# Down-weight sums in two places, and hand-overs written out by operation, in a two-layer encoder

## The chip, the core and the metric

One Trainium2 chip, of which the kernel uses one core. The metric is the device time of one launch in microseconds: 2563.12 as the median of three runs (2561.14 to 2563.65). One further execution was taken by the profiler; every duration and window below comes from that one.

## The reference

Two layers over 512 tokens of width 1024, all in float32. Each layer: a half-step FFN, a mixer, a second half-step FFN, each between two RMS norms.

```python
y = swiglu(rmsnorm(h, ffn1_pre_g[l]), ffn1_w_gu[l], ffn1_w_down[l])
h = h + 0.5 * rmsnorm(y, ffn1_post_g[l])
u = rmsnorm(h, mix_pre_g[l])
qa, ka, va, qb, kb, vb, qc, kc, vc, gl = jnp.split(u @ w_in[l], split_at, axis=-1)
...
yb = jnp.einsum('bsnc,ncd->bsnd', branches, w_branch[l])
merged = jnp.sum(sigmoid(gl + b_gate[l]) * yb, axis=2)
h = h + rmsnorm(merged @ w_out[l], mix_post_g[l])
y = swiglu(rmsnorm(h, ffn2_pre_g[l]), ffn2_w_gu[l], ffn2_w_down[l])
h = h + 0.5 * rmsnorm(y, ffn2_post_g[l])
```

`swiglu` is silu(gate) times up, times the down weights; the inner width is 2816. The three branches are a neighbourhood attention (a), a sliding-window attention with rotary (b) and a differential attention with rotary (c).

## The kernel before, in words

**Products in three.** Every float32 operand is split into a high part (a rounding copy by ScalarE) and a low part (the remainder, by VectorE), and a product is three matmuls: high by high, high by low, low by high (`mm3`, L298 to L300, and `unit` in the down part, L1014). Weights stream from DRAM in tiles of 512 KB through three raw buffers (`wr`, L186), are split by L199 and L200, and are used in the order of the list `order`.

**An FFN** has a gate and up part and a down part. Both use a scheme of seven products in place of eight on 2x2 blocks. In the gate and up part the first columns (`plain`: six in the first FFN, four in the others) go by ordinary products; then 16 or 18 groups of seven products each follow (L796, 84 matmuls of 256 columns per group), with `p1, p7, p6, p4, p2, p5, p3` in a written order. The sums of weight blocks that the seven products need are made by VectorE in each group (`sum13` L649, `sum2` L668, `sum4` L678).

**The down part** (from L868) works through units: `seq` lists kinds 1, 7, n2, 6, 4, n1, 2, 5, 3 with four units each (three in n1 and n2, which are ordinary products of the remaining rows). A unit of the seven takes one 512 KB tile of weights, split by `prep` (L892 and L893) some units ahead (`preps(s + 5)`), loaded by SP (`load`, L882) into three raw buffers and a ring of four. Kinds 7, 6, 5, 3 need sums of weight blocks: s3 = 21 + 11, s2 = s3 + 22, s1 = 21 + 22, s4 = s2 + 12. Before, all four are made in DRAM by transfers: a copy, and a second transfer that adds in flight (`sum_up`, L246 to L261; 32 transfers of 512 KB per FFN). They are issued on POOL, in small lots, each behind a one-column copy (`paced`, the mark of L265) that waits for a tile of the current work: for the first FFN of layer 0 two at a time within its own gate and up part (`beside`), for the second FFN of a layer and the first of the next layer spread over the mixer that lies ahead. Layer 0's mixer carries 64 such transfers, layer 1's 32.

The products land in PSUM banks for token blocks of 128: `a` and `c` in four banks, `b` in the seeds of the gate and up part, `d` and `e` in two more. Their sums are four quarters of y (two token blocks by 512 columns each): v11 (from b), v21, v22 and v12, kept in SBUF. `jobs` says at which unit such a step is issued.

**The hand-over** (`Handover`, L409) turns y into the next stage's operand, token block by token block: `take` squares and sums (ScalarE) and multiplies by the gain (VectorE, L436); `merge` makes the reciprocal root (L440 to L442), adds to the residual h (L450), squares h (L453), writes h to DRAM (`kept`, L468), and scales (L473); `turn` transposes on TensorE (L483) and splits the result (L487, L488; L492 keeps a plain copy). After the last FFN it transposes h instead (L458) and writes the output. `begin` starts the next stage with its first three column blocks, first for token blocks 0 and 1, then for 2 and 3, with hooks between its steps. The last mixer product (`w_out`) has a hand-over of the same class.

**What sets the order.** Outside `ordered()` a planner orders the instructions of each engine by its own costs. Inside (from the end of the gate and up part to the end of `begin`, and from `w_out` to the end of its `begin`) TensorE, ScalarE and VectorE keep the written order. Every engine takes its instructions in order, and so do the queues of SP and POOL. In the mixer POOL also does the rotary's multiplication (L1267), on a copy whose 32-row pieces SP has moved (`sh`, L1264), and adds the branches.

Of the kernel before, what the change touches and what calls it, by code (L numbers as in the profile page):

```python
# [16 lines left out]
P = 128  # L17
L = 2
# [91 lines left out]
def encoder_kernel(ctx: ExitStack, tc: tile.TileContext, order, xT, wts, cols, rows, rpb, consts, tables, out):  # L110
# [135 lines left out]
    def sum_up(l, which):  # L246

        steps = []

        def begin_sum(key, old, u):  # L250
            t = dr.tile([P, 2, T], F32, tag="sum", name=nm("sum"), bufs=L * 2 * 4 * (KS // 2))
            G.dma_start(t, down[l, which, (old, u)] if old == "21" else sums[l, which, (old, u)])
            sums[l, which, (key, u)] = t

        def add_to(key, more, u):
            G.dma_start(sums[l, which, (key, u)], down[l, which, (more, u)], accum_op=ALU.add, max_dma_last_dim=4096)

        for key, old, more in (("s3", "21", "11"), ("s2", "s3", "22"), ("s1", "21", "22"), ("s4", "s2", "12")):
            steps.extend((lambda key=key, old=old, u=u: begin_sum(key, old, u)) for u in range(KS // 2))
            steps.extend((lambda key=key, more=more, u=u: add_to(key, more, u)) for u in range(KS // 2))  # L260
        return steps  # L261
# [107 lines left out]
    def begin(X, first, spare, tags, hooks=(), between=None):  # L369
# [6 lines left out]
        assert len(held) <= len(spare)  # L376
        accs, ws = dense(first, X, tags, 0, hooks=dict(hooks))
        if between:
            between()
        dense(first, X, (), 1, accs, ws)  # L380
        return accs
# [27 lines left out]
    class Handover:  # L409


        def __init__(self, l, post, factors, following, gains, hold, value, raw, tags):
            self.tags = tags
# [8 lines left out]
            self.ss = [small("sh", 2, 8) for _ in range(NT)]  # L422
# [10 lines left out]
        def take(self, tb, n, src):  # L433
            junk = big("t", name="junk")
            A.activation(junk, src, AF.Square, accum_out=self.ss[tb][:, n : n + 1])
            V.tensor_tensor(out=self.value(tb, n), in0=src, in1=self.g1[n], op=ALU.mult)  # L436

        def rms(self, ss):
            r = small("rh", 1, 8)
            V.tensor_tensor(out=r, in0=ss[:, 0:1], in1=ss[:, 1:2], op=ALU.add)  # L440
            A.activation(r, r, AF.Sqrt, scale=1.0 / D, bias=epst)
            V.reciprocal(out=r, in_=r)  # L442
            return r

        def merge(self, tb):
            r = self.rms(self.ss[tb])
            s2 = small("sh", 2, 8)
            for n in range(2):
                y, h = self.value(tb, n), self.hold(tb, n)
                V.scalar_tensor_tensor(out=h, in0=y, scalar=r, in1=h, op0=ALU.mult, op1=ALU.add)  # L450
                if self.following:
                    junk = big("t", name="junk")
                    A.activation(junk, h, AF.Square, accum_out=s2[:, n : n + 1])  # L453
            if not self.following:
                for n in range(2):
                    tp = bank(self.tags[n])
                    for k in range(HB):
                        PE.transpose(tp[:, k * P : (k + 1) * P], self.hold(tb, n)[:, k * P : (k + 1) * P], ident)  # L458
                    o = self.value(tb, n)
                    (A.activation(o, tp, AF.Copy) if n else V.tensor_copy(o, tp))  # L460
                    nc.sync.dma_start(
                        out[n * T : (n + 1) * T, tb * P : (tb + 1) * P].rearrange("(k p) t -> p k t", p=P),
                        o.rearrange("p (k t) -> p k t", k=HB),
                    )
                return
            d = dr.tile([P, D], F32, tag="kept", name=nm("kept"), bufs=2 * NT)
            for n in range(2):
                nc.sync.dma_start(d[:, n * T : (n + 1) * T], self.hold(tb, n))  # L468
            kept[tb] = d
            r = self.rms(s2)  # L470
            for n in range(2):
                x = self.value(tb, n)
                V.scalar_tensor_tensor(out=x, in0=self.hold(tb, n), scalar=r, in1=self.g2[n], op0=ALU.mult, op1=ALU.mult)  # L473

        def turn(self, tb):
            if self.X is None:
                self.X = Operand(self.raw)
            raws = []
            for n in range(2):
                x = self.value(tb, n)  # L480
                tp = bank(self.tags[n])
                for k in range(HB):
                    PE.transpose(tp[:, k * P : (k + 1) * P], x[:, k * P : (k + 1) * P], ident)  # L483
                src = tp.rearrange("p (k t) -> p k t", k=HB)
# [4 lines left out]
                if self.raw:  # L489
                    raws.append((self.X.raw[n][:, tb // 2, :, ts], src))  # L490
            for o, src in raws:
                A.activation(o, src, AF.Copy)  # L492
# [22 lines left out]
    def ffn(l, which, X, accs):  # L515
# [37 lines left out]
        if first:  # L553
            stream["stop"] = len(order) // HB + 4 * plain
            accs = begin(X.blocks, firsts_of(l, 0), [spare("ht1"), spare("lt1")], ("mm", "at"), (), between)
            stream["beside"] = sum_up(l, which)
# [315 lines left out]
        done = {"load": 0, "prep": 0}  # L872
        place_of = {"1": "11", "2": "12", "4": "22", "7": "s3", "6": "s2", "5": "s1", "3": "s4", "n1": "n1", "n2": "n2"}

        def load(s):
            kind, u = seq[s]
            if s < UNITS:
                wraw[s] = sb.tile([P, 2, T], F32, tag="wr", name=nm("wr"), bufs=BUFS["wr"])
            else:
                wraw[s] = z(("ht3", "lt3", "ht2", "lt2")[s % 4], F32)  # L880
            key = place_of[kind], u
            nc.sync.dma_start(wraw[s], (sums if key[0][0] == "s" else down)[l, which, key])  # L882

        def prep(s):
            kind, u = seq[s]
            src = wraw.pop(s)
# [4 lines left out]
            else:  # L891
                A.activation(h, src, AF.Copy)  # L892
                V.tensor_tensor(out=q, in0=src, in1=f(h), op=ALU.subtract)  # L893
            wsplit[s] = h, q

        def loads(n):
            while done["load"] < min(n, len(seq)):
                load(done["load"])
                done["load"] += 1

        def preps(n):
            while done["prep"] < min(n, len(seq)):
                loads(done["prep"] + 1)
# [37 lines left out]
        for g in range(count):  # L941
# [49 lines left out]
            if g == count - 2:  # L991
                cut("1", "11", 1)
                loads(3)
# [5 lines left out]
        loads(6)  # L999
# [44 lines left out]
        def copies(name, tag, accs):  # L1044
            if tag:
                kept_v[name] = z(tag, F32)
# [4 lines left out]
        following = ("mix_pre_g", l) if which == 1 else ("ffn1_pre_g", l + 1) if l + 1 < L else None  # L1051

# [3 lines left out]
        def open_hand():  # L1056
# [3 lines left out]
            def value(tb, n):  # L1060
# [5 lines left out]
                    which == 2, ("mm", "mm"),  # L1066
                )
            )

        def first_rows():  # L1070
            t = z("ap", F32, (P, KP, T))
            kept_v["v11"], kept_v["v12"] = t[:, 0:2, :], t[:, 2:4, :]
            for tb in range(2):
                hand[0].take(tb, 0, b[tb])

        def second_rows():
            plus("v22", a)
            copies("v12", None, a)
            for tb in (2, 3):
                hand[0].take(tb, 1, kept_v["v22"][:, tb - 2, :])  # L1080
# [26 lines left out]
        job("n1", 2, lambda: [hand[0].take(tb, 1, kept_v["v21"][:, tb, :]) for tb in range(2)])  # L1107
        job("5", 0, first_rows)
        job("5", 1, lambda: hand[0].merge(0))
        job("5", 3, lambda: hand[0].merge(1))  # L1110
        job("3", 0, second_rows)

        for s, (kind, u) in enumerate(seq):
            for call in jobs.get(s, ()):
                call()
            loads(s + 8)
            preps(s + 5)
# [24 lines left out]
            elif kind == "3" and u == 0:  # L1142
                preps(len(seq))
                forms["3"] = forms["3x"]
                stream["eng"] = nc.sync
                turns = [lambda tb=tb: hand[0].turn(tb) for tb in range(NT)]
                if following:
                    ensure(stream["made"] + 2)
                    turns[0]()
                for tb in range(2):  # L1150
                    for i in range(UNITS):
                        seven(s + i, e, False, True, (tb,))
                        if following and tb == 0 and i == 1:
                            turns[1]()
                    t = kept_v["v12"][:, tb, :]
                    V.tensor_tensor(out=t, in0=e[tb], in1=t, op=ALU.add)
                    hand[0].take(2 + tb, 0, t)
                    hand[0].merge(2 + tb)
                    if following:
                        ensure(stream["made"] + 1)  # L1160
        if following:
            def held():
                t = pair("w").rearrange("p a (b c) -> p a b c", c=P)
                return t[:, 0], t[:, 1]

            if which == 2:
                stream["stop"] = len(order) // HB + 4 * 4
# [425 lines left out]
```

## Time and profile before

| | |
|---|---|
| median of three runs | 2563.12 us |
| the profiled execution: whole time | 2575.61 us |
| its span, first to last instruction | 2573.8 us |
| mean granted TensorE clock | 0.977 |
| DRAM read, written | 335.50 MB, 81.79 MB |

The profiler numbers lines as in the listing. "Busy" is time in which an engine computes; waiting, branching and issuing transfers don't count. A wait is put down to the operation that ended last before it. The granted clock is the share of TensorE's full rate that was allowed; it is 1 or 0.5 in any moment, so a mean of 0.86 is a stretch of which 28% ran at half rate. In a chain, each line is a piece of work with its start and its length, following back from the last one to what released it.

The stages of the profiled execution, from the change in TensorE's lines: first FFN of layer 0 to 373 us, its mixer to 945, second FFN to 1301; first FFN of layer 1 to 1653, its mixer to 2202, second FFN to the end.

### The profile page before, as it was taken

The page shows a single profiled execution, that of the slowest core. Times are in us where ns is not written, and L with a number is a line of the kernel's source. Part 1 is how long each engine was busy: PE and PEld are TensorE (multiplying, and loading weights), DVE is VectorE, ACT ScalarE, POOL GpSimd, SP SyncE. Part 2 cuts the span into 40 slices and gives each one's busy share as a digit, 9 for nine tenths or more (in the row PEclk, how much of TensorE's full clock was granted, in tenths as well). Part 3 has the DMA queues.
Part 4 walks back from the last instruction along what each step waited for, and adds up shares of the span by engine and source line. Part 5 has one row for each costly group of instructions (what it writes and reads, how often), then busy time and mean ns, then how long its engine had stood idle before and what let it go on. Part 6 is the DMA issues. An engine that isn't in the chain of part 4 may idle for free.

```text
span 2573.8 us, 37991 instructions
## 1 busy us (share of the span) xinstructions
PE 2454.7 (95%) x14298; PEld 2147.6 (83%) x14298; DVE 1766.9 (69%) x2903; ACT 1350.9 (52%) x2471; POOL 212.6 (8%) x304
## 2 busy tenths in 40 slices
PE   8999989999899999999989999899999999999997
PEld 7899878787777879998879998788877778899986
DVE  7687864756556567887668877667576574688784
ACT  5455644645444455555555555456454453556553
POOL 1121000121113200000000000000111121000000
PEclk9999999999999999999999999999999999999998
DMA  5686636677558533335523346365565553233452
GB/s 190 172 212 198 212 112 202 181 197 196 164 145 232 132 114 99 108 107 204 172 83 107 107 134 235 114 198 132 166 175 152 139 147 123 82 107 109 130 204 82
DMA packets 129432, 390.94 MB, mean 152 GB/s; under 512 B 17504, under 2 KB 24288, under 8 KB 128224
## 3 DMA queue, kind: packets, MB, share of 16 engines
q1 hardware_dynamic: 95952, 241.63, 30.0%
q0 software_dynamic: 11264, 67.12, 10.8%
q10 hardware_dynamic: 22032, 79.78, 9.9%
q8 instruction: 112, 1.84, 0.3%
q14 instruction: 72, 0.59, 0.1%
HBM read 335.50 MB, written 81.79 MB: 162 GB/s over the span
## 4 chain that ended last, share of the span: by engine, by line
PE 72%; DVE 10%; DMA 8%; ACT 5%; SPq 2%; issue 2%; POOL 1%; ACTq 0%; DVEq 0%; POOLq 0%
PE mm L796 22%; PE mm L1014 7%; PE mm L300 7%; PE mm L298 7%; PE mm L299 7%; PE at L1014 4%; PE at L796 4%; DMA sh<-raw 3%; PE at L300 2%; PE at L299 2%; PE at L298 2%; DMA wr<-in_wts_dram 2%; DMA braw<-in_rpb_dram 2%; PE o L1014 2%; DVE w L200 1%
## 5 line engine op out<-in xcount | busy, mean ns | idle before, releaser
L298 PE MATMUL mm<-X,w 128*128 128x512 f32 (+1 forms) x998 | 387.9, 389 | 3.0 <-ACT w L199 3.0
L299 PE MATMUL mm<-X,w 128*128 128x512 f32 (+1 forms) x998 | 388.3, 389 | 0.1
L300 PE MATMUL mm<-X,w 128*128 128x512 f32 (+1 forms) x998 | 387.5, 388 | 0.0
L200 DVE TENSOR_TENSOR w<-wr,w 128x512 fp32r<-128x512 f32 x366 | 257.7, 710 | 167.1 <-ACT w L199 163.4
L199 ACT ACTIVATE w<-wr 128x512 fp32r<-128x512 f32 x366 | 226.7, 627 | 240.3 <-PE mm L300 181.6
L796 PE MATMUL mm<-ht,h 128*128 128x256 f32 x1120 | 316.6, 283 | 2.4 <-ACT at L835 2.4
L796 PE MATMUL mm<-ht,l 128*128 128x256 f32 x1120 | 316.6, 283 | 0.0
L796 PE MATMUL mm<-lt,h 128*128 128x256 f32 x1120 | 315.7, 282 | 0.0
L298 PEld LDWEIGHTS mm<-X,w 128*128 128x128 f32 x998 | 192.1, 193 | 34.7 <-ACT w L199 3.4
L300 PEld LDWEIGHTS mm<-X,w 128*128 128x128 f32 x998 | 192.0, 192 | 32.2
L299 PEld LDWEIGHTS mm<-X,w 128*128 128x128 f32 x998 | 192.1, 192 | 31.9 <-DVE X L547 0.3
L796 PEld LDWEIGHTS mm<-ht,h 128*128 128x128 f32 x1120 | 213.5, 191 | 2.6 <-ACT at L835 2.6
L796 PEld LDWEIGHTS mm<-ht,l 128*128 128x128 f32 x1120 | 213.5, 191 | 0.0
L796 PEld LDWEIGHTS mm<-lt,h 128*128 128x128 f32 x1120 | 213.2, 190 | 0.0
L796 PE MATMUL mm<-X,h 128*128 128x256 f32 x1120 | 200.6, 279 | 3.5 <-DVE v L850 3.5
L1014 PE MATMUL mm<-wh,f 128*128 128x512 f32 x640 | 201.1, 392 | 0.0
L796 PEld LDWEIGHTS mm<-X,h 128*128 128x128 f32 x1120 | 171.0, 189 | 4.4 <-DVE v L850 4.1
L796 PE MATMUL mm<-X,l 128*128 128x256 f32 x560 | 155.3, 277 | 0.0
L265 POOL COPY mark<-w 128x1 f32<-128x1 f32 x96 | 26.1, 272 | 1421.3 <-DVE w L200 1418.7
L1014 PEld LDWEIGHTS mm<-wh,f 128*128 128x128 f32 x640 | 120.3, 188 | 26.8
L657 DVE TENSOR_TENSOR l<-wr,h 128x1024 fp32r<-128x1024 f32 x70 | 85.7, 1224 | 74.7 <-PE mm L796 74.6
L1014 PE MATMUL mm<-wl,f 128*128 128x512 f32 x320 | 126.2, 394 | 3.1 <-DVE wl L893 3.1
(353 smaller groups left out, 5617.3 us busy)
## 6 DMA issues: line engine op xcount, KB each, us to landing
wr<-in_wts_dram SPq DMA_DIRECT2D x187, 512.0 KB, 3.6
wr<-in_wts_dram ACTq DMA_DIRECT2D x152, 512.0 KB, 4.1
sum<-in_wts_dram POOLq DMA_DIRECT2D x96, 512.0 KB, 7.4
sum<-sum POOLq DMA_DIRECT2D x32, 512.0 KB, 5.2
ht<-sum SPq DMA_DIRECT2D x32, 512.0 KB, 4.4
lt<-sum SPq DMA_DIRECT2D x32, 512.0 KB, 4.1
ht<-in_wts_dram SPq DMA_DIRECT2D x28, 512.0 KB, 4.6
lt<-in_wts_dram SPq DMA_DIRECT2D x28, 512.0 KB, 3.6
```

The lines of the kernel that those rows point to most:

```text
L199: A.activation(hi, raw, AF.Copy)
L200: V.tensor_tensor(out=lo, in0=raw, in1=f(hi), op=ALU.subtract)
L265: mark = G.tensor_copy(small("mark", 1, 2), src)
L298: PE.matmul(acc, w[0], x[0], start=start, stop=False)
L299: PE.matmul(acc, w[0], x[1], start=False, stop=False)
L300: PE.matmul(acc, w[1], x[0], start=False, stop=stop)
L657: V.tensor_tensor(out=W[g]["l1"], in0=raws[g][0], in1=f(W[g]["h1"]), op=ALU.subtract)
L796: PE.matmul(acc, ws[i], xs[j], start=start and k == n == 0, stop=stop and k == HK - 1 and n == 2, skip_group_check=True,)
L1014: PE.matmul(acc, x[i], w[j], start=start and n == 0, stop=stop and n == 2, skip_group_check=True)
```

## The change

Four things.

- *Sums.* `sum_up` makes only s3 and s1 by transfers (16 per FFN). They are issued in the FFN's own gate and up part in all four FFNs, one behind each group instead of two, and in the plain columns only from m = 4 on. s2 and s4 are made by VectorE in `prep`: a kind 6 weight adds block 22 to the raw s3 in place, a kind 2 weight then adds block 12 to it. The raw s3 stays in the former ring of four; the other loads go through the three raw buffers and three slots of the tile `ap`, each issued behind the preparation that frees its place (`then`). Preparations run up to five units ahead by a table (`upto`).
- *Plain share.* `move_plain` adds the ordinary products' share `e` to `a` ahead of kind 5 and takes it off v22 again, so that kind 3 accumulates in `a` and needs no copy.
- *Hand-overs.* `take` and `merge` become single operations (square, root, gain, add, norm, transposes, split, plain copy), written out in the order in which each engine shall do them: token blocks 0 and 1 finish within kind 5 (`first_rows`), blocks 2 and 3 by `early` and `late`, with the splits of the block before put between. The mean of a row comes from the two half sums through the bias of the root. The banks of the transposes are fixed.
- *Weights.* The next stage's first weights are announced ahead (`announce`), fetched by SP within the down part and split in units 23 to 25 and before kind 3's products.

```diff
-        def begin_sum(key, old, u):
+        def begin_sum(key, u):
...
-        for key, old, more in (("s3", "21", "11"), ("s2", "s3", "22"), ("s1", "21", "22"), ("s4", "s2", "12")):
+        for key, more in (("s3", "11"), ("s1", "22")):
...
         def beside(src):
             if stream["beside"]:
-                paced(stream["beside"][:2], src)
-                del stream["beside"][:2]
+                paced(stream["beside"][:1], src)
+                del stream["beside"][:1]
...
-            beside(acts[m][:, 0:1])
+            if m > 3:
+                beside(acts[m][:, 0:1])
...
+        then = {
+            0: ("1", 3), 1: ("n2", 0), 2: ("n2", 1), 3: ("n2", 2), 8: ("4", 0), 9: ("4", 1), 10: ("4", 2),
+            15: ("n1", 2), 16: ("2", 0), 17: ("2", 1), 18: ("2", 2, 0), 19: ("2", 3, 1), 20: ("5", 0, 2),
+            24: ("5", 1, 0), 25: ("5", 2, 1), 26: ("5", 3, 2),
+        }
...
+            if kind == "6":
+                V.tensor_tensor(out=src, in0=src, in1=wraw[base["4"] + u], op=ALU.add)
             h, q = pair("wh"), pair("wl")
...
+            if kind == "2":
+                V.tensor_tensor(out=sigma[u], in0=sigma[u], in1=src, op=ALU.add)
             wsplit[s] = h, q
+            if s in then:
+                load(*then[s])
+            elif following and 21 <= s <= 23:
+                fetch(1, nc.sync)
...
+        def move_plain():
+            for i in range(2):
+                share, v = big("t", name="share"), kept_v["v22"][:, i, :]
+                A.activation(share, e[i], AF.Copy)
+                V.tensor_tensor(out=a[i], in0=a[i], in1=share, op=ALU.add)
+                V.tensor_tensor(out=v, in0=v, in1=share, op=ALU.subtract)
...
+        upto = {7: 11, 8: 12, 9: 13, 10: 14, 26: 30, 27: 30, 28: 30, 29: 32, 30: 32}
...
-            loads(s + 8)
-            preps(s + 5)
+            preps(upto.get(s, s + 5))
...
+            if 23 <= s < 26:
+                more_weights(1 if s < 25 else 2)
...
+                add22_(0)
                 preps(len(seq))
...
+                add22_(1)
+                H.turn(0)
+                H.early(2, 1, v22[:, 0, :])
+                evict(0)
+                H.early(3, 1, v22[:, 1, :])
+                more_weights(2)
+                H.plain(0)
+                for i in range(UNITS):
+                    seven(s + i, a, False, True, (0,))
+                H.turn(1)
+                H.late(2, 0, a[0], lambda: None, lambda: evict(1))
+                H.plain(1)
+                for i in range(UNITS):
+                    seven(s + i, a, False, True, (1,))
+                if not following:
+                    H.turn(2)
+                    evict(2)
+                    H.late(3, 0, a[1])
+                    H.turn(3)
+                    evict(3)
...
+            def second_block():
+                H.turn(2)
+                H.late(3, 0, a[1], lambda: None, lambda: evict(2))
+                H.plain(2)
+
+            def last_block():
+                H.turn(3)
+                evict(3)
+                H.plain(3)
...
+        def late(self, tb, n, src, *between):
...
+            self.square(("y", tb, n), src)
+            self.root(("y", tb, 1 - n), ("y", tb, n))
+            self.gained(tb, n, src)
+            more()
+            self.over(("y", tb, n))
+            self.add(tb, 0, ("y", tb, n))
+            self.add(tb, 1, ("y", tb, n))
+            if self.following:
+                self.part(("h", tb, 0))
+                self.root(("h", tb, 0), ("h", tb, 1))
+                more()
+                self.over(("h", tb, 1))
+                for i in range(2):
+                    self.norm(tb, i)
...
     def mixer(l, op, first):
-        todo = sum_up(l, 2) + (sum_up(l + 1, 1) if l + 1 < L else [])
...
-            while todo and len(todo) * (len(steps) - 10) > (len(steps) - 10 - n) * todo_n:
-                ready.append(todo.pop(0))
-            if ready:
-                paced(ready, f(stream["tile"][1])[:, 0, 0:1])
...
+        product(1, range(KD))
+        H.late(0, 1, last[0], lambda: weights(1), lambda: None)
+        weights(1)
+        product(2, range(KD // 2))
+        H.turn(0)
+        product(2, range(KD // 2, KD))
+        H.late(1, 1, last[1], lambda: H.operand(0), lambda: weights(1))
+        H.plain(0)
+        weights(1)
+        product(3, range(KD // 2))
+        H.turn(1)
+        product(3, range(KD // 2, KD))
+        H.late(2, 1, last[2], lambda: weights(1), lambda: H.operand(1))
+        H.plain(1)
```

`evict` is `operand` (the split) or, after the last FFN, `result` (the copy out). `early` is square, gain and the half sum's scaling.

More of the change, by code (lines that the diff above doesn't have):

```diff
@@ L421, in __init__ @@
                 self.g2 = self.gain(gains[1], *following)
-            self.ss = [small("sh", 2, 8) for _ in range(NT)]
+            self.sums = {}
             for tb in range(NT):
@@ L431, in gain, with square @@
             return halves
-        def take(self, tb, n, src):
+        def square(self, key, src):
             junk = big("t", name="junk")
-            A.activation(junk, src, AF.Square, accum_out=self.ss[tb][:, n : n + 1])
-            V.tensor_tensor(out=self.value(tb, n), in0=src, in1=self.g1[n], op=ALU.mult)
[L438 to L443, printed above, removed]
@@ L475, in turn, with part, root, over @@
-        def turn(self, tb):
+            s = self.sums[key] = small("sh", 1, 24)
+            A.activation(junk, src, AF.Square, accum_out=s)
+        def part(self, key):
+            s = self.sums[key]
+            V.tensor_scalar(out=s, in0=s, scalar1=1.0 / D, scalar2=EPS, op0=ALU.mult, op1=ALU.add)
+        def root(self, early, late):
+            s = self.sums[late]
+            A.activation(s, s, AF.Sqrt, scale=1.0 / D, bias=self.sums[early])
+        def over(self, key):
+            s = self.sums[key]
+            V.reciprocal(out=s, in_=s)
@@ new lines, in gained, with early, add @@
+        def gained(self, tb, n, src):
+            V.tensor_tensor(out=self.value(tb, n), in0=src, in1=self.g1[n], op=ALU.mult)
+        def early(self, tb, n, src):
+            self.square(("y", tb, n), src)
+            self.gained(tb, n, src)
+            self.part(("y", tb, n))
+        def add(self, tb, n, r):
+            h = self.hold(tb, n)
+            V.scalar_tensor_tensor(out=h, in0=self.value(tb, n), scalar=self.sums[r], in1=h, op0=ALU.mult, op1=ALU.add)
+            if self.following:
+                self.square(("h", tb, n), h)
@@ L992, in ffn @@
                 cut("1", "11", 1)
-                loads(3)
+                for u in range(3):
+                    load("1", u)
             if g:
@@ L998, in ffn @@
         region.__enter__()
-        loads(6)
+        for u in range(UNITS):
+            load("7", u, "sum")
         p3(count - 1)
@@ L1161, in ffn, with add22_, evict @@
-        if following:
[L1162 to L1167, printed above, removed]
+                forms["3"] = forms["3x"]
+                H, v22 = hand[0], kept_v["v22"]
+                def add22_(i):
+                    V.tensor_tensor(out=v22[:, i, :], in0=a[i], in1=v22[:, i, :], op=ALU.add)
+                def evict(tb):
+                    (H.operand if following else H.result)(tb)
```

244 lines of the change are left out of this document (127 added, 117 removed).

## The prediction

> **What bounds the kernel now.** I read the head of the profile first, then the list of waits of TensorE, then busy time by stage.
>
> ```profile
> span 2573.8 us, 37991 instructions
> PE 2454.7 (95%) x14298; PEld 2147.6 (83%) x14298; DVE 1766.9 (69%) x2903; ACT 1350.9 (52%) x2471; POOL 212.6 (8%) x304
> ```
> ```profile
> PE at L298 <- ACT w L199: 11.0, 3, 3.7
> PE mm L483 <- ACT ap L1048: 10.6, 3, 4.5
> ```
>
> TensorE sets the time. Its matmuls stay the same in number, so only its idle time (119 us) and the stretches at a lowered clock can be won or lost. The two waits (total, times, longest) come three times each: they belong to the hand-overs behind the FFNs. Where the rest lies the stages show. Columns: window and its length, then busy us (count) of PE, PEld, DVE, ACT, POOL, the granted clock, DMA share, GB/s.
>
> ```profile
> 45.00:88.00 43.00, 38.96 (x177) 31.77 (x176) 29.12 (x36) 20.03 (x29) 10.44 (x9) 0.92 0.69 199
> 88.00:255.00 167.00, 161.14 (x1346) 160.28 (x1345) 129.92 (x162) 88.56 (x146) 30.46 (x39) 0.99 0.72 200
> 392.00:946.00 554.00, 522.63 (x2465) 427.00 (x2466) 334.85 (x747) 276.03 (x598) 99.97 (x157) 0.96 0.63 176
> 1672.00:2203.00 531.00, 510.63 (x2466) 417.27 (x2466) 334.95 (x747) 275.97 (x597) 71.31 (x93) 0.99 0.54 152
> 355.00:392.00 37.00, 27.59 (x150) 24.26 (x148) 23.95 (x46) 17.29 (x43) 0.00 (x0) 0.86 0.31 112
> 1283.00:1321.00 38.00, 29.00 (x154) 24.86 (x152) 24.16 (x45) 21.15 (x48) 0.00 (x0) 0.87 0.25 84
> 1635.00:1672.00 37.00, 28.81 (x156) 25.45 (x154) 23.75 (x45) 17.57 (x43) 0.00 (x0) 0.86 0.32 107
> 946.00:968.00 22.00, 17.93 (x110) 16.11 (x108) 13.08 (x27) 12.20 (x31) 0.00 (x0) 0.84 0.27 87
> 2203.00:2225.00 22.00, 17.61 (x110) 15.74 (x107) 13.18 (x27) 12.21 (x30) 0.00 (x0) 0.84 0.28 93
> 2531.00:2573.80 42.80, 28.44 (x120) 22.17 (x118) 19.40 (x32) 11.51 (x22) 0.00 (x0) 0.84 0.17 53
> 1005.00:1183.00 178.00, 178.00 (x1513) 178.00 (x1512) 142.26 (x178) 98.17 (x160) 0.00 (x0) 1.00 0.38 121
> 1183.00:1283.00 100.00, 99.22 (x434) 81.09 (x434) 72.45 (x77) 55.26 (x72) 0.00 (x0) 1.00 0.56 186
> ```
>
> The gate and up part (1005 to 1183) and the down part before its end (1183 to 1283) run without loss. What loses is the first layer's start, both mixers, five hand-overs and the end; each costs its idle time and then a lowered clock (length minus busy time, plus busy time by one minus the clock). The two mixers do the same work with the same matmuls, and layer 0's takes 23 us longer. What differs is the background transfers, first in layer 0's mixer, then in layer 1's (count, size, median us to landing):
>
> ```profile
> sum<-in_wts_dram POOLq DMA_DIRECT2D x48, 512.0 KB, 7.2
> sum<-sum POOLq DMA_DIRECT2D x16, 512.0 KB, 5.1
> ...
> sh<-raw SPq DMA_DIRECT2D x52, 64.0 KB, 4.4
> ```
> ```profile
> sum<-in_wts_dram POOLq DMA_DIRECT2D x24, 512.0 KB, 7.5
> ...
> sum<-sum POOLq DMA_DIRECT2D x8, 512.0 KB, 4.8
> sh<-raw SPq DMA_DIRECT2D x52, 64.0 KB, 3.1
> ```
>
> 64 transfers against 32, and the rotary's small transfer, for which the chain of a head waits, lands in 4.4 against 3.1 us.
>
> **The change, part by part.**
>
> *The mixers lose all their sum transfers* and the marks that go ahead of these on POOL, past which the rotary's multiplication (also POOL) had to queue. Layer 0's mixer should fall at least to layer 1's time: 23 us. That one loses 20.4 idle and about 5 by its clock (531 at 0.99). From its waits and its chain:
>
> ```profile
> PE at L1202 <- ACT x L1311: 9.7, 3, 5.7
> ```
> ```profile
> 1984.72 7.37 DMA sh<-raw
> ...
> 2037.42 5.53 DMA wr<-in_wts_dram
> ```
>
> The longest wait ends a chain with a rotary transfer of 7.37 us. At the 3.1 median it is 4.3 shorter; the second has a weight fetch of 5.53 in its chain, 2.0 above the 3.5 of a stage without sums (below). With half of the clock loss (2.5) that is 9 us more, in both mixers: 23 + 9 + 9 = 41. Bounds for the 9: nothing, if these waits have other causes, and 16, if two thirds of the 25 go.
>
> *The sums move to the gate and up part*, half as many, one per group instead of none; in layer 0's first FFN one instead of two, and from a later m on.
>
> ```profile
> 53.27 1.20 POOL L252 DMA_DIRECT2D sum<-in_wts_dram  x2
> ```
> ```profile
> 54.69 7.65 DMA kept<-h
> ```
> ```profile
> 95.89 7.28 DMA wr<-in_wts_dram
> ```
> ```profile
> wr<-in_wts_dram SPq DMA_DIRECT2D x31, 512.0 KB, 5.6
> ```
> ```profile
> wr<-in_wts_dram SPq DMA_DIRECT2D x37, 512.0 KB, 3.5
> ```
>
> Two sums were issued at 53.27, and a write of h that usually is short took 7.65; its buffer held up ScalarE and TensorE (45 to 88: 4.0 idle, 3.1 by the clock). No sum starts before m = 4 now, so 7 us go (0 to 7). At 95.89 a weight fetch took 7.28 beside two sums. At the rate of 1005 to 1183 (178 / 1513 a matmul) the 1346 of 88 to 255 take 158.4, so two sums a group cost 8.6 there. With one I take half back, 4.3 (0 to 8.6). In the three other FFNs one sum comes to each group of 9.9 us (178 over 18 groups), where fetches land in 3.5; even beside two sums their median was 5.6, well inside a group. I take 0.5 each (0 to 4.3, half the 8.6).
>
> *Two of the four sums are made by VectorE* in the down part: eight adds of 1024 columns per FFN. Durations from the groups of 1183 to 1321 (count, busy, mean ns), a piece of the chain with two squares and their reads, and the reciprocal square root's ACT step:
>
> ```profile
> L893 DVE TENSOR_TENSOR wl<-lt,wh 128x1024 fp32r<-128x1024 f32 x14 | 17.1, 1223 | 8.4 <-ACT wh L892 8.4
> ...
> L488 DVE TENSOR_TENSOR X<-mm,X 128x512 fp32r<-128x512 f32 x7 | 4.5, 685 | 5.3 <-ACT X L487 5.3
> ...
> L487 ACT ACTIVATE X<-mm 128x512 fp32r<-128x512 f32 x8 | 4.3, 590 | 4.2 <-PE mm L483 4.2
> ...
> L450 DVE SCALAR_TENSOR_TENSOR a<-ap,rh,a 128x512 f32<-128x512 f32 x4 | 3.0, 752 | 0.1
> ...
> L441 ACT ACTIVATE rh<-rh,eps 128x1 f32<-128x1 f32 x8 | 2.4, 295 | 4.8 <-DVE rh L440 4.7
> ```
> ```profile
> 1276.61 1.39 ACT junk L453 x4
> ```
> ```profile
> 2545.31 5.51 PE at L1014 x24
> ...
> 2567.72 1.95 PE mm L458 x8
> ```
>
> 8 x 1.22 = 9.8, four of them ahead of a ScalarE copy that VectorE then waits for (about 1 each, 4), and move_plain's four steps of 0.69 (2.8): 16.6 more on 72.45 of 100, so 89. A unit is 2.8 us (12 matmuls of 0.23, by the row of 24). In the densest four units (kind 6) VectorE has some 14 us in 11.1, but each prepared weight is due four units after it is asked for and the units before (n2) leave room: no wait, taken at 0.5 per FFN (0 to 4). The loads now follow single preparations on SP, each at least three units (8 us) ahead of its use, against 3.5 to 5.6 to land; queued behind them are the residual's rows and gains.
>
> *The hand-overs behind the FFNs* lose 13.3, 12.8 and 12.2 now (idle 9.4, 9.0, 8.2, the rest clock): 38.3. The next stage's first six weight pieces are fetched and split in units 23 to 25 and before token block 0 of kind 3, so the wait for w goes. move_plain puts e into a before kind 5, so kind 3 adds into a directly and the copy to ap (L1048) goes. What is late next, counted from the end of kind 5, each engine in its written order: VectorE has first_rows (two gains 1.4, four adds and four scalings 6.0, small ones 1, 1.4 of chain) and two splits (2.4), 12.2 against kind 5's 11.1 (48 matmuls), then add22_: TensorE may go on at +1.9, less about 1.0 for the transposes of block 0 (half of 1.95, which ran at a lowered clock): wait 0.9. Block 0 of kind 3 ends at 7.4, block 1 at 13.9. VectorE meanwhile: two splits, add22_, two early rows, one operand, two weights, one gain: about +10.1; then reciprocal and two adds 1.7, ScalarE's square 0.8 and root 0.3, copy 0.6, VectorE's 0.7: block 1's operand is there at 14.4, wait 0.5. The same count gives 0.3 before block 2's transposes and 1.0 before block 3's. That is about 3 in waits of at most 1 us each, and the clock should hold: 38.3 - 3 x 3 = 29.3. Bounds: 35, and 18 if each keeps 2 more in waits and the clock drops in part.
>
> *The mixer's own end* (946, 2203) loses 6.9 and 7.2. The same count there gives waits of 0.5, 2.3, 0.3 and 1.0 (block 0's operand and the early weights stand ahead of late in ScalarE's queue): 8.6 for both, so 5.5 of 14.1 would go if the clock held.
>
> ```profile
> PE at L298 <- ACT X L487: 2.3, 2, 2.0
> PE at L299 <- DVE X L488: 1.5, 1, 1.5
> ```
>
> Here waits of 2.0 and 1.5 were followed by 0.84 of the clock. My 2.3 is as long, so I leave the loss by clock in: 0 gained (-6 to 10). The Trainium skill ("TensorE: Matmul & The Clock Gate", section "Why this matters for your kernels") asks for no idle gaps over about 3 us; by it 2.3 would do no harm and 5.5 us would be gained. The trace doesn't agree, and I go by the row.
>
> *The end* (2531 to 2573.8): 14.4 idle, of which 4.1 lie behind the last transposes (2569.7) and stay; 4.5 by the clock. The transposes of blocks 0 and 1 leave kind 5 for places where their rows are long ready. After block 1 of kind 3 come block 2's transposes; block 3 then needs result copy 0.6, square 0.8, root 0.3, reciprocal 0.2, two adds 1.5: TensorE waits about 2.9 in place of 10.3. 7.4 and part of the clock: 10 (5 to 13).
>
> Sum: 41 + 7 + 4.3 - 1.5 - 2 + 29.3 + 0 + 10 = 88 us. The profiled execution took 2575.6 in all; it would come to 2487. The runs' median is 2563.1, half a per cent lower, and the same stages make it up: 2475.
>
> **Rivals.**
>
> *The sums stall the weight fetches (slower).* For it: 7.28 at 95.89 and the 8.6 us. If each of the 51 groups of the three other FFNs lost a quarter of 8.6, as the first two groups of layer 0 did, that is 110, and 34 in layer 0's own: 88 + 1.5 - 4.3 - 144 is 59 slower, 2622. It decides from where one fetch beside one sum takes longer than a group, 9.9. Against it: median 5.6 beside two.
>
> *The mixers' 23 us are not the transfers'* but, say, the first layer's buffers: 41 becomes 0, 2516. Against it: the counts of instructions are equal and the transfers' landing times differ.
>
> *The hand-overs only swap their waits:* ScalarE's strict order puts operand(1) behind late(2). The FFNs' gain falls to 12, the mixers' end costs 6, the end gives 5: 2503.
>
> *VectorE bounds the down part:* 16.6 more, if it finds no cover there, is up to 12 us of wait per FFN: 88 - 46 = 42, 2521.
>
> *The transfers just take their harm along* to the down part, because the last sums land late: gain near nothing, 2561.
>
> **How the numbers follow.** The forecast 0.60; stalled fetches 0.04; mixers 0.10; hand-overs 0.16; VectorE 0.07; nothing gained 0.03. A measurement of this kernel tells 0.2% (5 us) from no change. Faster: 0.60 + 0.10 + 0.16 + 0.07 = 0.93, same 0.03, slower 0.04. Range: the favourable ends together give 130, of which all at once is unlikely, so down to 2440; upwards the mixer and VectorE cases, 2525. Outside lie the slower case, the one without gain and the tails.
>
> **What would show it.** Right: no sum in the mixers, both within a few us of each other and below 525; rotary transfers landing at 3.1 or less; no w L199 and ap L1048 among TensorE's waits; hand-overs of 27 to 30 us in place of 37 and 38 at a clock near 1; gate and up parts of 178 to 180, and about 162 in the first. Wrong: gate and up parts over 185 with VectorE's r or ACT's h waiting for wr; L1014 waiting for wl by more than some us per FFN; layer 1's mixer still at 531.

## The result, and the profile after

The changed kernel takes 2442.8 us (median of four, 2441.6 to 2443.1) beside 2563.4 (2561.1 to 2580.2) for the kernel before on the same chip: a ratio of 0.9515, 95% interval 0.9475 to 0.9555, so faster by about 120 us. The forecast was 2475 with a range from 2440 to 2525. The median of 2442.8 lies near the range's lower end; by the ratio, the 2563.1 from which the forecast started becomes 2438.8, just below it: the kernel gained more than the prediction allowed. The direction was right; the gain between the medians, 120.6 us, is over a third larger than the 88 us of the sum. The profiled executions differ by 134 us (2575.6 and 2441.6); the one of before was a long one among its kind.

The head of the page after:

```profile
span 2439.8 us, 37786 instructions
PE 2404.1 (99%) x14298; PEld 2111.5 (87%) x14298; DVE 1797.8 (74%) x2943; ACT 1347.5 (55%) x2471; POOL 192.1 (8%) x192
```

The same matmuls are 50 us less busy (hardly any of them run at half rate now: the mean granted clock is 0.999 in place of 0.977), and TensorE is 36 us idle instead of 119. The stages after, each window cut at the same instructions as the windows of the prediction and in their order (window, length, busy PE, PEld, DVE, ACT, POOL, granted clock, DMA share, GB/s):

```profile
44.30:80.80 36.50, 36.45 (x177) 29.61 (x176) 30.83 (x38) 21.33 (x31) 0.77 (x2) 1.00 0.50 170
80.80:239.30 158.50, 158.50 (x1346) 158.46 (x1346) 127.88 (x161) 87.82 (x145) 24.88 (x30) 1.00 0.63 169
363.30:877.70 514.40, 506.16 (x2467) 414.61 (x2465) 335.10 (x752) 277.04 (x599) 43.19 (x29) 1.00 0.45 126
1571.70:2086.70 515.00, 506.77 (x2466) 414.49 (x2465) 335.09 (x752) 277.40 (x600) 43.57 (x29) 1.00 0.45 127
339.30:363.30 24.00, 22.80 (x149) 20.56 (x148) 18.93 (x34) 12.20 (x31) 0.00 (x0) 1.00 0.23 83
1208.20:1233.40 25.20, 23.89 (x157) 21.62 (x156) 20.23 (x36) 16.46 (x38) 0.00 (x0) 1.00 0.18 64
1546.80:1571.90 25.10, 23.91 (x157) 21.52 (x155) 20.02 (x36) 13.02 (x32) 0.00 (x0) 1.00 0.19 64
877.70:893.80 16.10, 14.68 (x108) 13.40 (x109) 12.03 (x23) 10.66 (x27) 0.00 (x0) 1.00 0.29 99
2086.70:2102.80 16.10, 14.82 (x109) 13.54 (x109) 12.03 (x24) 10.51 (x27) 0.00 (x0) 1.00 0.29 99
2408.20:2439.80 31.60, 24.58 (x120) 20.10 (x118) 17.75 (x29) 10.21 (x21) 0.00 (x0) 0.91 0.21 67
930.30:1108.30 178.00, 178.00 (x1514) 178.00 (x1513) 142.22 (x178) 97.67 (x160) 26.47 (x32) 1.00 0.61 165
1108.30:1208.30 100.00, 99.22 (x435) 81.19 (x434) 85.37 (x97) 59.60 (x84) 0.00 (x0) 1.00 0.48 165
```

Laid beside the sum of the prediction:

| term | forecast | before to after, us | measured |
|---|---|---|---|
| both mixers | 41 | 554.0 to 514.4, 531.0 to 515.0 | 55.6 |
| layer 0's start | 7 | 43.0 to 36.5 | 6.5 |
| layer 0's first gate and up part | 4.3 | 167.0 to 158.5 | 8.5 |
| three other gate and up parts | -1.5 | 178.0 to 178.0 | 0 |
| down parts | -2 | 100.0 to 100.0 | 0 |
| hand-overs behind FFNs | 29.3 | 37 to 24.0, 38 to 25.2, 37 to 25.1 | 37.7 |
| the mixers' ends | 0 | 22 to 16.1, twice | 11.8 |
| the end | 10 | 42.8 to 31.6 | 11.2 |
| sum | 88 | | 131 |

One of the three other gate and up parts and one of the four down parts is shown; the other two such gate and up parts run at the full clock without idle time as well (1268 to 1446 and 2137 to 2315 of the span). The remaining 3 of 134 lie in the few us between the windows. The largest waits of TensorE now (in all, times, longest):

```profile
PE o L1369 <- DVE lo L325: 5.2, 6, 1.4
PE mm L1082 <- DVE ht L1244: 3.7, 3, 1.3
...
PE at L512 <- DVE a L464: 2.8, 1, 2.8
```

The waits for w and for ap behind the FFNs are gone. L1244 is add22_, the wait of about 1 us that was forecast behind kind 5; L464 is the last block's add at the end, forecast as 2.9.

### The profile page after: what moved, and what is told of

Its sections match the earlier page's. It is cut to its first block, busy times and chain, and to the rows that moved or that the text cites. A ratio compares the mean times of both kernels' runs of the same rounds, so it can differ in the third digit from the quotient of the medians.

```text
span 2439.8 us, 37786 instructions
## 1 busy us (share of the span) xinstructions
PE 2404.1 (99%) x14298; PEld 2111.5 (87%) x14298; DVE 1797.8 (74%) x2943; ACT 1347.5 (55%) x2471; POOL 192.1 (8%) x192
## 5 line engine op out<-in xcount | busy, mean ns | idle before, releaser
L298 PE MATMUL mm<-X,w 128*128 128x512 f32 (+1 forms) x1044 | 397.1, 380 | 2.2 <-ACT w L199 1.7
L299 PE MATMUL mm<-X,w 128*128 128x512 f32 (+1 forms) x1044 | 396.8, 380 | 0.7 <-DVE X L522 0.7
L300 PE MATMUL mm<-X,w 128*128 128x512 f32 (+1 forms) x1044 | 396.1, 380 | 0.0
L200 DVE TENSOR_TENSOR w<-wr,w 128x512 fp32r<-128x512 f32 x360 | 255.3, 714 | 168.2 <-ACT w L199 167.0
L298 PEld LDWEIGHTS mm<-X,w 128*128 128x128 f32 x1044 | 197.4, 189 | 34.0 <-ACT w L199 1.9
L299 PEld LDWEIGHTS mm<-X,w 128*128 128x128 f32 x1044 | 197.2, 189 | 32.2 <-DVE X L522 1.1
L300 PEld LDWEIGHTS mm<-X,w 128*128 128x128 f32 x1044 | 197.1, 189 | 31.4
L324 ACT ACTIVATE hi<-at 128x256 fp32r<-128x256 f32 (+2 forms) x168 | 77.2, 474 | 73.4 <-PE at L1365 37.9
```

The costliest lines, as they stand in the source:

```text
L200: V.tensor_tensor(out=lo, in0=raw, in1=f(hi), op=ALU.subtract)
L298: PE.matmul(acc, w[0], x[0], start=start, stop=False)
L299: PE.matmul(acc, w[0], x[1], start=False, stop=False)
L300: PE.matmul(acc, w[1], x[0], start=False, stop=stop)
L324: A.activation(hi, src, AF.Copy)
```

## Experiments

Each kernel ran beside the kernel before, whose medians were 2570.3 (first four), 2569.4 (next four) and 2566.0 (last two). Times are medians.

**1. Only the place of the transfers.** The kernel before, with all four sums left to transfers, now in every FFN:

```diff
-            stream["beside"] = sum_up(l, which)
+        stream["beside"] = sum_up(l, which)
...
-        todo = sum_up(l, 2) + (sum_up(l + 1, 1) if l + 1 < L else [])
...
```

> The kernel before with one part of the change alone: all four sums stay transfers (32 per FFN, two behind each group), but every FFN issues them in its own gate and up part and the mixers carry none. Theory (the transfers of the mixers cost the 55 us that the mixers fell by): mixers at about 494 us between the end of begin and the end of w_out's first products (533 and 510 before), hand-overs as before; 2563 - 55 = 2508, plus 0 to 9 us for each of the three gate and up parts that now have two transfers per group: 2508 to 2535. Rival A (the mixers fell because of the new hand-overs and the planner's other order): mixers stay at 533 and 510, time 2563 or more. Rival B (two transfers per group stall the weight fetches): gate and up parts of 190 us and more in place of 178, time above 2545.

2531.6 us, ratio 0.9856 (0.9832 to 0.9879). Its mixers, cut like those above, and one of its later gate and up parts:

```profile
388.90:905.60 516.70, 508.10 (x2466) 415.70 (x2467) 335.25 (x747) 275.83 (x597) 42.98 (x29) 1.00 0.43 123
1638.80:2154.40 515.60, 506.89 (x2466) 414.63 (x2467) 333.95 (x747) 275.86 (x597) 43.29 (x29) 1.00 0.44 124
...
964.70:1146.70 182.00, 179.60 (x1512) 179.40 (x1511) 142.97 (x178) 96.92 (x161) 34.84 (x45) 0.99 0.73 205
```

Both mixers fall to what the changed kernel has (514.4 and 515.0) with the old hand-overs, so rival A falls. Two transfers per group cost these gate and up parts 2 to 5 us each, not stalls of 12: rival B falls too. 52.7 us are won in the mixers and some 11 given back; the time falls by 1.4%, clear of the noise. The hand-overs behind the FFNs keep the waits that they had, so what the changed kernel gains there isn't due to the place of the transfers:

```profile
PE mm L483 <- ACT ap L1048: 11.2, 3, 4.5
...
PE at L298 <- ACT w L199: 10.2, 3, 3.7
```

**2. The halved transfers back in the mixers.**

```diff
-        stream["beside"] = sum_up(l, which)
+        stream["beside"] = sum_up(l, which) if first else []
...
+        todo = sum_up(l, 2) + (sum_up(l + 1, 1) if l + 1 < L else [])
...
```

> The changed kernel with its 16 transfers per FFN put back into the mixers behind the marks of before: 32 in layer 0's mixer, 16 in layer 1's, none in the three later gate and up parts. Theory (transfers): layer 0's mixer at about 510 (what layer 1's had with 32 before), layer 1's at about 502, against 494: 2443 + 16 + 8 = 2467. Rival A (order of the planner, new hand-overs): both stay at 494, 2443. Rival C (it takes the crowding of 64): both stay within 3 us of 494, below 2450.

2458.2, 15 above the changed kernel (expected 24).

```profile
364.10:888.50 524.40, 509.81 (x2466) 416.38 (x2464) 336.12 (x751) 277.11 (x599) 71.13 (x93) 0.99 0.55 156
1582.50:2100.20 517.70, 506.41 (x2467) 414.09 (x2465) 334.94 (x751) 276.93 (x599) 57.98 (x61) 1.00 0.51 142
```

32 transfers cost 10 us here and 16 in layer 1 before; 16 cost 2.7; 64 cost layer 0 before 39.6. By these figures the harm grows faster than the number. They are rough: the changed kernel's own layer 0 mixer takes 514.4, 517.4 and 518.0 in three profiles (after and experiments 3 and 5), so the 10 could be 6. The median landing of the rotary's 64 KB goes with the transfers in layer 0's mixer: 2.0 without them (after), here 4.2 with 32.

```profile
sh<-raw SPq DMA_DIRECT2D x52, 64.0 KB, 2.0
```
```profile
sh<-raw SPq DMA_DIRECT2D x52, 64.0 KB, 4.2
```

In layer 1's mixer it doesn't: the median is 3.1 with the 32 transfers of before and 2.8 without any (3.1 and 3.4 in experiments 3 and 5). What falls there is the longest landing, from 7.1 to 4.8 (shortest, median, longest; before, then after), and with it the wait for x, from 9.7 in sum to 1.3:

```profile
DMA to landing us min/median/max: 1.9/3.1/7.1
```
```profile
DMA to landing us min/median/max: 1.9/2.8/4.8
```
```profile
PE at L1318 <- ACT x L1425: 1.3, 2, 1.1
```

**3. The marks without transfers.**

```diff
+            if ready:
+                paced([], f(stream["tile"][1])[:, 0, 0:1])
...
```

> The changed kernel with the marks of before in both mixers (a one-column copy on POOL that waits for the weight tile in use, at the places of before), but with no transfer behind them. Theory (transfers): mixers within 3 us of 494, 2443 to 2449. Rival D (the marks hold up POOL's queue, so the rotary's multiplication, or the release of the weight buffers): both mixers longer, up to 533 and 510, 2460 to 2498.

2444.3, against 2442.8 and 2443.0 for the changed kernel in two measurements: no measurable difference, and both mixers stay where they were.

```profile
364.20:881.60 517.40, 508.23 (x2466) 415.29 (x2465) 335.46 (x751) 277.30 (x599) 56.83 (x93) 1.00 0.44 125
1575.90:2091.00 515.10, 506.76 (x2466) 414.31 (x2465) 334.97 (x751) 277.10 (x599) 50.14 (x61) 1.00 0.45 127
```

The marks, and what they hold up in POOL's queue and the weight buffers, were not the cause; the transfers were.

**4. Two at a time in layer 0's first FFN.**

```diff
-                paced(stream["beside"][:1], src)
-                del stream["beside"][:1]
+                n = 2 if first else 1
+                paced(stream["beside"][:n], src)
+                del stream["beside"][:n]
...
-            if m > 3:
-                beside(acts[m][:, 0:1])
+            beside(acts[m][:, 0:1])
```

> The changed kernel, in which layer 0's first FFN issues its transfers two at a time and from m = 2 on, as before (16 in all, so for half as many groups). Theory (two transfers in flight hold up the writing of h and the first weight fetches): the start up to the gate and up part back from 80.6 to about 87.8 us, that part from 158.5 to 163 to 167; 2443 + 7 + 4 to 8 = 2454 to 2458. Rival (the start got shorter by the other order of the instructions): 2443.

2457.5, 14.5 more.

```profile
44.30:86.50 42.20, 38.44 (x180) 31.39 (x179) 29.91 (x37) 20.62 (x30) 10.38 (x9) 0.96 0.73 207
86.50:251.60 165.10, 160.28 (x1345) 159.88 (x1344) 129.89 (x162) 88.66 (x145) 11.89 (x15) 0.99 0.51 149
```
```profile
PE o L778 <- ACT h L780: 3.8, 1, 3.8
PE mm L842 <- DVE v L896: 3.6, 3, 2.6
...
PE mm L842 <- ACT at L881: 2.2, 1, 2.2
```
```profile
DVE r L695 <- DMA wr<-in_wts_dram: 9.5, 2, 5.7
```

Both losses of the first layer come back with their waits, 5.7 and 6.6 us: the wait for h, and two longer ones in the first groups (2.2 and 2.6), where VectorE waits for weight fetches, as its row from 80 to 110 us shows. In the changed kernel, with one transfer per group and a later start, the second loss isn't halved but gone. The run puts back both the pairs and the early start, so it doesn't tell which of the two matters.

**5. The changed kernel again** (to compare with 6 to 8).

> The changed kernel as it is, as the measure for the three runs beside it: 2443, within 3 us.

2443.0 (2441.7 to 2446.3), ratio 0.9510 (0.9493 to 0.9527).

**6. The next stage's weights split late.**

```diff
         def more_weights(n):
-            if following:
-                ensure(stream["made"] + n)
+            pass
```

> The changed kernel in which the next stage's weights are still fetched within the down part, but split only when its first products ask for them (no splits in units 23 to 25 nor before kind 3). Theory (the early splits are one of the things that empty the hand-over, and a wait of 3 us or more also lowers the clock): behind each of three FFNs the wait for w of 3 to 4 us comes back with up to 3 us by the clock, 60.8 and 38.6 us become 65 to 68 and 43 to 46; 2443 + 12 to 21 = 2455 to 2464. Rival (the new order of late alone emptied them, the splits find room anyway): within 2 us, below 2446.

2455.8, 12.8 more, at the lower end of what the theory gave. Its hand-over behind layer 1's first FFN, TensorE's waits and then the clock behind them:

```profile
PE at L300 <- DVE ht L200: 1.9, 1, 1.9
PE at L300 <- DVE w L200: 1.4, 1, 1.4
```
```profile
1582.00:1587.00 5.00, 5.00 (x31) 5.00 (x31) 1.73 (x3) 1.19 (x2) 0.00 (x0) 0.66 0.34 105
```

The wait for w returns in two pieces (1.4 and 1.9, where 3.7 was one piece before), and the clock drops. The early splits are thus worth a third of the 37.7 us. The other two thirds belong to move_plain and the new order of the steps together; no run takes these two apart.

**7. VectorE's sums doubled.** Each sum is followed by a step of the same size that leaves it as it is:

```diff
+                V.tensor_tensor(out=src, in0=src, in1=src, op=ALU.max)
...
+                V.tensor_tensor(out=sigma[u], in0=sigma[u], in1=sigma[u], op=ALU.max)
```

> The changed kernel with a second step of 1.22 us behind each of VectorE's eight sums per FFN (the maximum of the sum with itself, which changes nothing). Theory (VectorE has room in the down part, the eight sums cost nothing): down parts at 100.1 to 101, 2443 to 2447. Rival (VectorE is at its limit there, so that a further 9.8 us per FFN show): down parts of 105 to 110, 2463 to 2480.

2457.5, 14.5 more: between the two expectations. Of 39 us of added VectorE work 14.5 show: 1.5 us in the down part up to kind 5 that is shown here (101.5 beside 100.0), and more behind it, where the wait for add22_ adds up to 10.8 in place of 3.7:

```profile
1113.80:1215.30 101.50, 99.92 (x436) 81.12 (x435) 92.72 (x103) 57.06 (x82) 0.00 (x0) 1.00 0.47 162
```
```profile
PE mm L1084 <- DVE ht L1246: 10.8, 3, 3.7
PE mm L1084 <- DVE wl L960: 6.2, 8, 0.8
```

**8. Two steps put later.** The preparation of kind 3's second weight goes behind add22_(0), and at the end the copy of block 2 behind late(3):

```diff
-        upto = {7: 11, 8: 12, 9: 13, 10: 14, 26: 30, 27: 30, 28: 30, 29: 32, 30: 32}
+        upto = {7: 11, 8: 12, 9: 13, 10: 14, 26: 30, 27: 30, 28: 30, 29: 31, 30: 31}
...
                     H.turn(2)
-                    evict(2)
                     H.late(3, 0, a[1])
+                    evict(2)
```

> The changed kernel with two steps put later: kind 3's second weight is prepared behind add22_(0) instead of before it, and at the end block 2's rows are copied out behind late(3) instead of before it. Theory (the 1.2 to 1.3 us that are left behind kind 5 are VectorE's queue, and at the end ScalarE's copy stands ahead of the last square): 3 x 1.1 and 1 to 1.4 us less, 2443 - 4.5 = 2438.5. Rival (the second weight then comes late to its unit): the first wait shrinks but a wait for wl of about 1 us takes its place, 2442.

2436.9 (2436.6 to 2437.7), ratio 0.9485 (0.9469 to 0.9500), and 6.1 us under the changed kernel measured beside it. The wait for L1244 shrinks from 3.7 in sum to 0.3, and the one at the end from 2.8 to 1.5, 4.7 us together:

```profile
PE at L512 <- DVE a L464: 1.5, 1, 1.5
...
PE mm L1082 <- DVE ht L1244: 0.3, 1, 0.3
```

So this version beats both kernels.

**9. VectorE's sums left out.**

```diff
-            if kind == "6":
-                V.tensor_tensor(out=src, in0=src, in1=wraw[base["4"] + u], op=ALU.add)
...
-            if kind == "2":
-                V.tensor_tensor(out=sigma[u], in0=sigma[u], in1=src, op=ALU.add)
```

> The changed kernel without VectorE's eight sums per FFN: it leaves them out, so kinds 6 and 3 multiply by other weights. Theory (the first eight sums use up VectorE's room in the down part and show only as the wait of 1.2 us behind kind 5): 3 x 1.2 = 3.6 us less, 2443 - 3.6 = 2439.4, down parts still at 100.1. Rival A (they are hidden entirely and that wait has another cause): 2443. Rival B (they cost as much as the second eight, 13 to 14 us): 2429.

2443.1: no gain, rival A. The theory fell: the wait behind kind 5 stays, and is longer.

```profile
PE mm L1078 <- DVE ht L1240: 5.2, 3, 1.7
```

The first eight sums are hidden entirely; why the wait grows by 0.5 was not settled.

**10. The split ahead of late.**

```diff
                 H.turn(1)
-                H.late(2, 0, a[0], lambda: None, lambda: evict(1))
+                evict(1)
+                H.late(2, 0, a[0])
```

and the same for block 2.

> The changed kernel in which, behind the FFNs, a block's transposes are split at once and late of the next block comes after, in place of the split standing between late's two roots. Theory (the written order of these steps is what keeps the waits short): two splits go ahead of late, whose chain ends 1 to 2 us later, so that TensorE waits for the rows of block 2 or 3: 3 x 1 to 2 us, 2446 to 2449. Rival (there is slack, any order does): 2443, within 1.5.

2445.1, at most 2 more (expected 3 to 6), which the spread of the changed kernel's own runs (2441.6 to 2446.3) covers. One small wait is new in the list:

```profile
PE at L512 <- DVE ap L477: 1.3, 3, 0.5
```

The order of these two matters little; most of what I put on it is slack.

## Where the prediction failed, and what of it held

The step that failed is the sum. The parts that it named are the ones that gained, but nearly every term was too small, the mixers' above all: 41 became 55.6. The mixers' ends were put at 0 and gave 11.8, the hand-overs gave 37.7 for 29.3, the first gate and up part 8.5 for 4.3, and the 3.5 us of cost in the gate and up parts and the down parts didn't come. Together that is 131 for 88. The range failed with it: "the favourable ends together give 130, of which all at once is unlikely, so down to 2440". They did come all at once. The terms weren't independent: most of them held back a part of the loss by clock, and the clock rose in all these stages together, to 0.999 in the mean.

*Mixers.* Right in cause: experiment 1 gives the whole gain by moving the transfers alone, experiment 3 excludes the marks. Wrong in size: "that is 9 us more, in both mixers" measured 16 in each (55.6 - 23 = 32.6 for both). I took the shortening of two waits and half the clock loss. In fact 12.2 of layer 1's 20.4 us of idle time went, and 3.9 of about 5 by the clock (TensorE busy 510.6 before, 506.8 after). Experiments 2 and 1 show 10 and 16 us for 32 transfers; I had allowed at most 16 as a bound and taken little more than half of it. The reasoning behind the 9 was half right: in layer 1's mixer the waits do end in rotary transfers, but their median landing stays near 3; the long ones went (experiment 2).

*Layer 0's first gate and up part.* "With one I take half back, 4.3" measured 8.5. The cost isn't proportional to the transfers: it lies in the waits of the first groups, which are there with pairs and an early start (experiment 4) and absent in the changed kernel. Which of the two decides stays open. The start's 7 was right (6.5; experiment 4 brings 5.7 back).

*Hand-overs behind the FFNs.* "That is about 3 in waits" measured 1.2 to 1.3, and the clock held as forecast. Counting VectorE's queue, I added full durations. The timeline after shows neighbours overlapping:

```profile
1214.48 0.68 DVE L522 TENSOR_TENSOR X<-mm,X 128x512 fp32r<-128x512 f32 x1
1215.08 0.68 DVE L455 TENSOR_TENSOR ht<-ht,ht 128x512 f32<-128x512 f32 x1
...
1215.74 0.68 DVE L200 TENSOR_TENSOR ht<-wr,ht 128x512 fp32r<-128x512 f32 x1
1216.34 0.68 DVE L200 TENSOR_TENSOR lt<-wr,lt 128x512 fp32r<-128x512 f32 x1
```

Steps of 0.68 start 0.60 apart. Over some 20 steps that is 1.6 us by my estimate, about what the later three of the four waits (0.5, 0.3, 1.0) come to; that they went for this reason is argued, not shown. The first one, 0.9, was there with 1.2 to 1.3; experiment 8 shows that most of it is the preparation queued ahead of add22_. The rest of the difference (37.7 against 38.3 less waits of 3.7) is how I priced the clock. I took busy time by one minus the mean clock, but the mean is taken over the whole window: 14% of 37, 13% of 38 and 14% of 37 us make 15.3, where I had 11.7. With the 26.6 idle and less 3.7 that gives 38.2, beside the 37.7 measured.

*The mixers' ends.* "I leave the loss by clock in: 0 gained" measured 11.8. The count of 4.3 in waits (its four add up to 4.1) was too long, perhaps for the same reason; the windows after leave 1.4 and 1.3 idle, and their longest wait is 0.8. So the question whether a wait of 2.3 lowers the clock didn't arise there, and neither the row nor the Trainium skill's 3 us was tested by it. I had also read the row too narrowly: its two waits stand one behind the other with 0.4 us of work between them, so it doesn't show what a single wait of 2.3 does.

```profile
951.75 0.38 PE L298 MATMUL at<-X,w 128*128 128x256 f32 x1 [2.04 <-ACT X L487]
953.60 0.58 PE L299 MATMUL at<-X,w 128*128 128x256 f32 x1 [1.47 <-DVE X L488]
```

*VectorE in the down part.* "No wait" was right: with the sums, VectorE is busy 85 of 100 us (89 forecast) and the part takes the same 100.0; leaving them out gains nothing (experiment 9). The margin is small: a second eight would cost 14.5 (experiment 7).

*The end.* 2.9 forecast for the wait, 2.85 measured; 11.2 for 10.

*The rivals.* Stalled fetches (slower) fell: none of the later gate and up parts lost time, and even two transfers per group cost 2 to 5 us each. (That rival counts 51 groups where three times 18 are 54; it would come to about 2628, and nothing hangs on it.) That the hand-overs only swap their waits fell with their windows: 24.0 to 25.2 us, with one wait of 1.2 to 1.3 left in each. "The mixers' 23 us are not the transfers'" fell with experiment 1, and that the harm moves along with the transfers fell with the unchanged stages.

## What to carry to other kernels

Look for stages that do the same work under different background load: the difference between layer 0's and layer 1's mixer was the whole diagnosis, and extrapolating it to no load should go through the lighter stage's remaining waits, all of them. Bulk transfers belong in a stage whose own loads are prefetched, not in one whose chain waits for small transfers. When counting an in-order queue by hand, take the distance between starts from a timeline, not the durations. Price a lowered clock over the whole window that its mean is taken from. And when several terms hang on the same loss, let the range allow that they all come at once.

## What the runs showed of the hardware that was not expected

Waits of about the same length sometimes lower TensorE's clock and sometimes don't. In experiment 6, the hand-over shown had no wait above 1.9 us, and a stretch at half rate followed (0.66 over the 5 us above); behind layer 0's second FFN its longest wait was 1.3, and the clock from 1238 to 1243 us was 0.66 as well. In experiment 7 the three waits behind kind 5 are 3.6, 3.5 and 3.7 us long. The first, which ends at 345 us, left the clock at 1; the third, which ends at 1564, didn't:

```profile
PE mm L1084 <- DVE ht L1246: 3.6, 1, 3.6
```
```profile
340.00:360.00 20.00, 16.39 (x90) 13.80 (x89) 17.31 (x30) 11.95 (x26) 0.00 (x0) 1.00 0.19 64
1558.60:1578.60 20.00, 16.33 (x77) 13.42 (x76) 16.79 (x29) 11.84 (x26) 0.00 (x0) 0.91 0.20 67
```

The rule that the Trainium skill gives ("TensorE: Matmul & The Clock Gate", section "Why this matters for your kernels": no idle gaps over about 3 us) is thus too generous for experiment 6 and drew no line in experiment 7. What decides between the two cases was not settled.

The spread of the runs also fell when the transfers left the mixers: 2561 to 2580 for the kernel before, 2530.6 to 2534.7 for it with the transfers moved, 2441.6 to 2446.3 for the changed one. Experiment 6, with no transfers in the mixers, spreads over 6 us too (2455.7 to 2461.8), so the transfers are at most a part of it; this was not tested by itself.
